# Weight subtractions, softmax scalings and unit-block additions on VectorE instead of GpSimd

## The chip, the core and the metric

The kernel runs on one NeuronCore of a Trainium2 chip. A core has a matmul engine (TensorE, PE in the rows; its weight loads are PEld), three engines for elementwise work (VectorE = DVE, ScalarE = ACT, GpSimd = POOL), a queue engine (SyncE = SP) and 16 DMA engines. The engines run their own instruction lists in order and wait for each other through semaphores. SBUF is the on-chip working memory, PSUM the memory into which TensorE writes its products. The metric is the device time of one execution in microseconds.

## The reference

Two transformer blocks run one after the other on 256 tokens of width 1024 in f32. Cut to what matters:

```python
# first block (16 meta tokens are put ahead of the 256)
z = rmsnorm(h, g_pre_mix) @ w_in
attn = sliding_window_attention_with_sinks(q, k, v, sinks)    # 8 heads of 64
hr = rg_lru(causal_depthwise_conv(xr), ...)                   # a scan along the tokens
h = h + rmsnorm(concat(attn, gelu(yr) * hr) @ w_out, g_post_mix)
h = h + rmsnorm(square(relu(rmsnorm(h, g_pre_ffn) @ w_ff1)) @ w_ff2, g_post_ffn)
# second block
proj = rms_norm(h, ln_pre_mix) @ w_in_2                       # 1024 -> 9232
y_a = moba_attention(rope(q_a), rope(k_a), v_a)               # 8 heads of 128
y_b = rms_norm(gated_delta_rule(q_b, k_b, v_b, g, beta)) * silu(z)   # a triangular solve per 64 tokens
merged = sigmoid(gate_a) * (y_a @ w_proj_a) + sigmoid(gate_b) * (y_b @ w_proj_b)
h = h + rms_norm(merged @ w_out_2, ln_post_mix)
h = h + rms_norm((silu(f @ w_gate) * (f @ w_up)) @ w_down, ln_post_ffn)   # f = rms_norm(h)
return h + sigmoid(h @ w_ple_gate) * rms_norm(p @ w_ple, ln_ple)
```

## The kernel before, in words

**Weights in two halves.** Every large product is computed as three matmuls in a reduced f32 format (fp32r): an operand x is split into `hi`, x rounded to fp32r, and `lo`, the rest x - hi, and the product is hi·hi + hi·lo + lo·hi (`mm3`). The weights arrive as 258 chunks of 128 x 1024, one DMA each, into a tile `raw` (4 buffers). `prep` splits a chunk in two halves of 512 columns; for each, a copy makes `whi` (ScalarE, sometimes VectorE, in the rows CAST) and a subtraction makes `wlo`. These are the 516 subtractions of the kernel: 436 on VectorE, 80 on GpSimd. Up to 9 chunks may be prepared ahead of the one in use. A chunk feeds 24 matmuls of 256 columns or 12 of 512.

**What sets the order.** The program is written out by a planner. Each call to an engine goes through `Timed` (so every row of the profile shows its line, 111), which moves a `Clock` of estimated times per engine and per tile. TensorE's list is mainly the weight stream. Between its pieces `tick` lets "side streams" (generators: attention, the delta rule, norms) advance when the Clock says that their tiles are ready, and `prefetch` prepares further chunks when the Clock's ACT, DVE and DMA times are not too far ahead of TensorE's. A change of the engine that does a step changes the estimates, and by them the place of many other steps in all lists.

**The steps that the change touches.** `split` gives a subtraction to GpSimd when GpSimd could start it more than 0.5 us (`PLO`) earlier than VectorE by the Clock. `softmax4` is used by both attentions: scores with mask into SBUF, row maximum, exponentials on ScalarE, reciprocal of the sum, then a scaling of four blocks, two of them on GpSimd. `gdn` is the delta rule of one pair of heads (four pairs, 0 to 3): GpSimd inverts 16 x 16 unit blocks by a chain of 14 pairs of small operations (`tmp`, `g`), sends them through DRAM into `cmp`, adds the unit diagonal (`cmp` + `eye`), and VectorE makes `Z` of it; GpSimd also makes the product `gm` for the next pair's decay, clears half of a tile `Q` (MEMSET) and computes powers (`aq`, `rk`, `ro`).

**Other names.** `u` is a normalised row block at the boundary between stages: VectorE makes it from `h`, a factor `ms` (a power, computed by GpSimd) and a gain, and TensorE transposes it into `uT`, on which the next weights act. `rope` multiplies a q or k pair by cosines and sines on VectorE (three rows `g<-ps,cst`), and GpSimd adds the two parts; `gl` holds the delta rule's log decays.

Of the kernel before, what the change touches and what calls it, by code (L numbers as in the profile page):

```python
# [8 lines left out]
F32 = mybir.dt.float32  # L9
# [39 lines left out]
WARM, KEEP = 8, (1, 1)  # L49
DHI, PLO, DCP = 0.0, 0.5, 1.0  # L50
FIRST = "x0 x1 x2 x3 k0 k1 q0 q1 y0 y1"
# [5 lines left out]
class Clock:  # L57
    """Estimated time of each engine and of each tile, by which the order of the program is chosen."""

# [27 lines left out]
class Soon(tuple):  # L87
    """Tiles that a stage of a side stream waits for, where it may be placed a little ahead of them."""


def parts_of(x):
    """Names under which the clock keeps a tile: the transposed operands in parts, others as a whole."""
    n = x.tensor.name
    if not n.startswith("uT"):
        return [n]
    dims = [d[1] for d in x.ap[1:]]
    (k, c), m = divmod(x.offset, TM), dims[0] if len(dims) > 1 else 1
    return [f"{n}.{i}.{j}" for i in range(k // 4, (k + m - 1) // 4 + 1) for j in range(c // P, (c + dims[-1] - 1) // P + 1)]


class Timed:
    """An engine whose calls also move the estimated times."""

# [41 lines left out]
def griffin_then_moba_gdn_kernel(ctx: ExitStack, tc, a, out):  # L145
# [54 lines left out]
    def copy(dst, src):  # L200
        on_dve = start_of("dve", src) + (DCP if src.tensor.name in clk.bank else DHI)
        if on_dve < start_of("act", src):
            dve.tensor_copy(dst, src)
        else:
            act.activation(dst, src, AF.Copy)

    def hilo(src, hi, lo, eng=None):
        copy(hi, src)
        (eng or dve).tensor_tensor(lo, src, hi.bitcast(F32), op=SUB)
# [21 lines left out]

# [1 line left out]
    jobs, posts, sides = [], [], []  # L233
# [17 lines left out]
    def split(i, j, src, hi, lo):  # L251
        if i < 2:
            return hilo(src, hi, lo, dve if (i, j) == (0, 1) else pool)
        copy(hi, src)
        eng = pool if start_of("pool", hi) + PLO < start_of("dve", hi) else dve
        eng.tensor_tensor(lo, src, hi.bitcast(F32), op=SUB)

# [87 lines left out]

# [1 line left out]
    def gain(n, scale=None, eng=dma):  # L347
# [80 lines left out]
    def tok_split(groups, after=None, cut=()):  # L428
        """Column groups of a product whose operand is still being made, token tile 0 before token tile 1."""
        def fn():  # L430
# [120 lines left out]
    def softmax4(parts, scale, sink, norm):  # L551
# [19 lines left out]
        for k, x in enumerate(norm):  # L571
            eng = pool if k < 2 else dve
            eng.tensor_scalar(x, x, sm[:, k:k + 1], None, op0=MUL)
        yield norm

# [1 line left out]
    hh = [hp.tile([P, D], F32, name=f"h{t}") for t in range(2)]  # L577
# [120 lines left out]

# [1 line left out]
    w1 = a["w1in"]  # L700
# [190 lines left out]

# [1 line left out]
    def hm4(t, r, hms):  # L893
# [57 lines left out]

# [1 line left out]
    beta, hbeta, gl, xx, eg, es = (small(n, (P, 2, 8)) for n in ("beta", "hbeta", "gl", "xx", "eg", "es"))  # L953
# [197 lines left out]
    def gdn(f, p):  # L1151
# [62 lines left out]
        yield cmp, aq  # L1214
        pool.tensor_tensor(cmp, cmp, bc4(C("eye")), op=ADD)
        dve.tensor_scalar(aq, aq, float(P) ** -0.5, None, op0=MUL)
# [128 lines left out]

# [1 line left out]
    def first2(hms):  # L1347
# [54 lines left out]

# [1 line left out]
    def fin(j):  # L1404
# [113 lines left out]
```

## Time and profile before

| | before |
|---|---|
| device time, three runs | 877.6, 879.09 (median), 881.04 us |
| profiled execution, first to last instruction | 878.8 us |
| TensorE busy | 849.5 us (97%) |
| VectorE busy | 610.7 us (69%) |
| ScalarE busy | 447.1 us (51%) |
| GpSimd busy | 278.1 us (32%) |
| mean granted TensorE clock | 0.992 |

The profiled execution's span lies 0.3 us below the median of the three runs. Busy time of TensorE is modelled at its ends, so 97% doesn't say that it streams all the time. The shares are means over stages that differ: 17 to 104 us is the first block's mixer, 123 to 295 its feed-forward part, 323 to 658 the second block's mixer, 663 to 856 its feed-forward part, and short boundaries lie between them.

### The profile page before, as it was taken

The numbers are of one execution on the slowest core, as the hardware profiler recorded it, in microseconds if no ns is written. First come the engines' busy times: TensorE is split into PE (matmuls) and PEld (weight loads), VectorE is DVE, ScalarE is ACT, GpSimd is POOL, SyncE is SP. The second block draws the span as 40 slices with busy tenths as digits, with TensorE's granted clock in tenths as the row PEclk, the third lists the DMA queues.
The fourth block names the chain that finished last, engine by engine and source line by source line (L and its number), as shares of the span: only waits on it lengthen the run. The fifth ranks groups of instructions, "written<-read, shape, count | busy, mean of one in ns | idle before, by whom it ended". The sixth has DMA issues, their size and how long they took to land.

```text
span 878.8 us, 15562 instructions
## 1 busy us (share of the span) xinstructions
PE 849.5 (97%) x5905; PEld 778.6 (89%) x5905; DVE 610.7 (69%) x1047; ACT 447.1 (51%) x995; POOL 278.1 (32%) x345
## 2 busy tenths in 40 slices
PE   8989989999999998899989999899999999999997
PEld 7978769999999788899989999899977999999977
DVE  6996887555555658988879998756758756645463
ACT  6855656554455454456444454346446545544441
POOL 4523321111111234454474758611223112311121
PEclk9999999999999999999999999999999999999999
DMA  7633737766665246444543335325553867565511
GB/s 275 232 124 116 253 106 255 240 186 185 184 189 191 74 165 212 131 143 130 201 132 122 99 107 193 114 88 172 183 168 129 270 199 268 190 197 187 188 53 49
DMA packets 47773, 147.19 MB, mean 167 GB/s; under 512 B 9281, under 2 KB 10561, under 8 KB 47698
## 3 DMA queue, kind: packets, MB, share of 16 engines
q1 hardware_dynamic: 47554, 146.13, 51.1%
q8 instruction: 46, 0.75, 0.3%
q14 instruction: 29, 0.24, 0.1%
q10 hardware_dynamic: 144, 0.07, 0.0%
HBM read 143.82 MB, written 2.36 MB: 166 GB/s over the span
## 4 chain that ended last, share of the span: by engine, by line
PE 73%; DVE 13%; POOL 6%; issue 4%; ACT 2%; DMA 2%; SPq 0%; DVEq 0%; POOLq 0%; ACTq 0%
PE ps L111 73%; DVE g L111 5%; DVE wlo L111 4%; POOL g L111 2%; POOL tmp L111 1%; DVE u L111 1%; DVE whi L111 1%; POOL sp_p L111 1%; ACT whi L111 1%; ACT junk L111 1%; DMA raw<-in_ff1t 1%; POOL wlo L111 1%; DVE s_m L111 1%; DMA g<-in_pT 0%; DMA raw<-in_w2q 0%
## 5 line engine op out<-in xcount | busy, mean ns | idle before, releaser
L111 PE MATMUL ps<-uT,whi 128*128 128x256 f32 (+1 forms) x2272 | 419.9, 286 | 0.0
L111 DVE TENSOR_TENSOR wlo<-raw,whi 128x512 fp32r<-128x512 f32 x436 | 320.3, 771 | 89.0 <-ACT whi L111 85.4
L111 PEld LDWEIGHTS ps<-uT,whi 128*128 128x128 f32 x2272 | 353.7, 190 | 4.7 <-issue 1.2
L111 ACT ACTIVATE whi<-raw 128x512 fp32r<-128x512 f32 x477 | 270.8, 623 | 110.1 <-issue 58.8
L111 PE MATMUL ps<-uT,wlo 128*128 128x256 f32 (+1 forms) x1136 | 320.4, 282 | 0.0
L111 PEld LDWEIGHTS ps<-uT,wlo 128*128 128x128 f32 x1136 | 216.4, 191 | 0.0
L111 POOL TENSOR_TENSOR wlo<-raw,whi 128x512 fp32r<-128x512 f32 x80 | 113.4, 1422 | 319.5 <-ACT whi L111 309.3
L111 PE MATMUL ps<-whi,hm 128*128 128x512 f32 x432 | 138.6, 393 | 0.0
L111 ACT ACTIVATE g<-ps 128x512 f32<-128x512 f32 (+4 forms) x104 | 51.6, 509 | 136.2 <-PE ps L111 132.1
L111 PEld LDWEIGHTS ps<-whi,hm 128*128 128x128 f32 x432 | 81.2, 188 | 17.4
L111 PE MATMUL ps<-g 128*128 128x128 f32 (+9 forms) x560 | 76.3, 287 | 11.2 <-POOL g L111 5.7
L111 PE MATMUL ps<-wlo,hm 128*128 128x512 f32 x216 | 84.9, 393 | 0.0
L111 PEld LDWEIGHTS ps<-g 128*128 128x128 f32 (+5 forms) x560 | 64.5, 181 | 17.8 <-POOL g L111 6.3
L111 PE MATMUL ps<-whi,uT 128*128 128x512 f32 (+1 forms) x256 | 74.6, 371 | 0.8 <-DVE uT L111 0.7
L111 PEld LDWEIGHTS ps<-whi,uT 128*128 128x128 f32 x256 | 45.5, 188 | 11.3 <-DVE uT L111 2.6
L111 POOL TENSOR_TENSOR g<-g 128x512 f32<-128x512 f32 (+1 forms) x20 | 30.6, 1531 | 72.7 <-DVE g L111 67.9
L111 PEld LDWEIGHTS ps<-wlo,hm 128*128 128x128 f32 x216 | 40.6, 188 | 8.3
L111 PE MATMUL ps<-wlo,uT 128*128 128x512 f32 (+1 forms) x128 | 46.9, 366 | 0.0
L111 DVE SCALAR_TENSOR_TENSOR g<-ps,vec,g 128x255 f32<-128x255 f32 (+5 forms) x84 | 35.0, 475 | 7.2 <-ACT g L111 6.9
L111 POOL TENSOR_TENSOR ms<-ms,mhalf 128x1 f32<-128x1 f32 (+1 forms) x19 | 11.7, 614 | 65.4 <-DVE ms L111 65.3
L111 ACT ACTIVATE junk<-ps 128x128 bf16<-128x128 f32 (+1 forms) x48 | 17.9, 384 | 27.5 <-PE ps L111 27.5
L111 ACT ACTIVATE hm<-g 128x512 fp32r<-128x512 f32 x23 | 14.6, 633 | 33.2 <-DVE g L111 33.2
(168 smaller groups left out, 905.2 us busy)
## 6 DMA issues: line engine op xcount, KB each, us to landing
raw<-in_ff SPq DMA_DIRECT2D x60, 512.0 KB, 4.4
raw<-in_w2qkv SPq DMA_DIRECT2D x24, 512.0 KB, 4.0
raw<-in_ffdown SPq DMA_DIRECT2D x22, 512.0 KB, 4.0
raw<-in_ffg SPq DMA_DIRECT2D x18, 512.0 KB, 4.3
raw<-in_ffu SPq DMA_DIRECT2D x18, 512.0 KB, 3.7
raw<-in_w1in SPq DMA_DIRECT2D x14, 512.0 KB, 3.6
raw<-in_w1out SPq DMA_DIRECT2D x8, 512.0 KB, 3.5
gain<-in_rows SPq DMA_DIRECT2D x16, 256.0 KB, 5.4
```

The lines of the kernel that those rows point to most:

```text
L111: r = call(*args, **kw)
```

## The change

Three kinds of operations go from GpSimd to VectorE: all subtractions for `wlo` but three in the first two chunks, the scaling of the first two blocks in `softmax4`, and the addition of the unit diagonal to `cmp`. The constant `PLO` goes with the rule that used it. Comments are dropped too.

```diff
-DHI, PLO, DCP = 0.0, 0.5, 1.0
+DHI, DCP = 0.0, 1.0
...
     def split(i, j, src, hi, lo):
-        if i < 2:
-            return hilo(src, hi, lo, dve if (i, j) == (0, 1) else pool)
-        copy(hi, src)
-        eng = pool if start_of("pool", hi) + PLO < start_of("dve", hi) else dve
-        eng.tensor_tensor(lo, src, hi.bitcast(F32), op=SUB)
+        hilo(src, hi, lo, pool if i < 2 and (i, j) != (0, 1) else dve)
...
         for k, x in enumerate(norm):
-            eng = pool if k < 2 else dve
-            eng.tensor_scalar(x, x, sm[:, k:k + 1], None, op0=MUL)
+            dve.tensor_scalar(x, x, sm[:, k:k + 1], None, op0=MUL)
...
         yield cmp, aq
-        pool.tensor_tensor(cmp, cmp, bc4(C("eye")), op=ADD)
+        dve.tensor_tensor(cmp, cmp, bc4(C("eye")), op=ADD)
```

Counted over the whole lists, VectorE's `wlo<-raw,whi` rows go from 436 to 513 and GpSimd's from 80 to 3; 16 scalings (8 of 128 x 128, 4 of 128 x 144, 4 of 128 x 256) and 4 additions of 128 x 64 change engine; and 8 `whi` copies that were VectorE's become ScalarE's, because the Clock now sees VectorE later. By stage, the 77 moved subtractions are 5 more on VectorE up to the end of the first mixer, 18 in the first feed-forward part, 27 in the second mixer, 25 in the second feed-forward part and 2 at the end. TensorE's and the DMA queue's instructions keep their number.

GpSimd's list from the end of the first mixer to the start of the second; `ms` is the power for a norm, of which each boundary has four. The difference of the lists:

```order
 L111 TENSOR_TENSOR g<-g 128x512 x4
-L111 TENSOR_TENSOR wlo<-raw,whi 128x512
-L111 TENSOR_TENSOR ms<-ms,mhalf 128x1 x4
-L111 TENSOR_TENSOR wlo<-raw,whi 128x512 x18
-L111 TENSOR_TENSOR ms<-ms,mhalf 128x1 x2
-L111 TENSOR_TENSOR wlo<-raw,whi 128x512
-L111 TENSOR_TENSOR ms<-ms,mhalf 128x1 x2
-L111 TENSOR_TENSOR wlo<-raw,whi 128x512 x2
+L111 TENSOR_TENSOR ms<-ms,mhalf 128x1 x8
 L111 TENSOR_TENSOR sp_s<-sp_s,sp_e 128x16
```

At both boundaries GpSimd is left with the eight powers alone.

GpSimd's list in the second mixer, where the small chain of head pair 0 ends and the `gm` of the next pair follows. Before:

```order
L111 TENSOR_TENSOR g<-g,cst 128x512
L111 TENSOR_TENSOR aq<-sq,mhalf 128x4
L111 TENSOR_TENSOR wlo<-raw,whi 128x512 x2
L111 TENSOR_TENSOR gm<-glr_106,cst 128x512
L111 TENSOR_TENSOR gm<-glr_107,cst 128x512
L111 TENSOR_TENSOR cmp<-cmp,cst 128x64
L111 MEMSET g 128x16x16
L111 TENSOR_TENSOR wlo<-raw,whi 128x512 x3
L111 TENSOR_TENSOR rk<-sk,mhalf 128x4
```

The same place after the change:

```order
L111 TENSOR_TENSOR g<-g,cst 128x512
L111 TENSOR_TENSOR aq<-sq,mhalf 128x4
L111 TENSOR_TENSOR gm<-glr_106,cst 128x512
L111 TENSOR_TENSOR gm<-glr_107,cst 128x512
L111 MEMSET g 128x16x16
L111 TENSOR_TENSOR rk<-sk,mhalf 128x4
```

The two subtractions ahead of `gm`, the addition behind it and three subtractions ahead of `rk` are gone.

VectorE's list at the second mixer's start, from the key's `rope` of the first attention pair (three products with `cst`) through that pair's softmax. Before:

```order
L111 TENSOR_TENSOR wlo<-raw,whi 128x512 x6
L111 TENSOR_TENSOR g<-ps,cst 128x512
L111 TENSOR_TENSOR g<-ps,cst 64x512 x2
L111 TENSOR_TENSOR wlo<-raw,whi 128x512 x5
L111 TENSOR_TENSOR g<-ps,cst 128x512
L111 TENSOR_TENSOR g<-ps,cst 64x512 x2
L111 SCALAR_TENSOR_TENSOR g<-ps,cst 128x256
L111 TENSOR_REDUCE s_m<-g 128x2
L111 SCALAR_TENSOR_TENSOR g<-ps,cst 128x512
L111 TENSOR_REDUCE s_m<-g 128x2
L111 TENSOR_SCALAR s_m<-s_m 128x4
L111 TENSOR_TENSOR wlo<-raw,whi 128x512 x2
```

After the change, from the row that follows that key's `rope`:

```order
L111 TENSOR_TENSOR wlo<-raw,whi 128x512 x4
L111 SCALAR_TENSOR_TENSOR g<-ps,cst 128x256
L111 TENSOR_REDUCE s_m<-g 128x2
L111 SCALAR_TENSOR_TENSOR g<-ps,cst 128x512
L111 TENSOR_REDUCE s_m<-g 128x2
L111 TENSOR_SCALAR s_m<-s_m 128x4
L111 TENSOR_TENSOR g<-ps,cst 128x512
L111 TENSOR_TENSOR g<-ps,cst 64x512 x2
L111 CAST whi<-raw 128x512
L111 TENSOR_TENSOR wlo<-raw,whi 128x512 x2
L111 RECIPROCAL s_r<-s_r 128x4
L111 TENSOR_SCALAR g<-g,s_r 128x128 x2
```

Between the query's `rope` and the key's stand 3 subtractions where there were 6; between the key's `rope` and the scores stand 4 where there were 5, and the next pair's query `rope` has moved behind the scores. The two scalings of 128 x 128 are new on this engine.

## Rows read from the trace of the kernel before

**Rows 1.** The page's first part: busy us, share of the span, instructions.

```profile
PE 849.5 (97%) x5905; PEld 778.6 (89%) x5905; DVE 610.7 (69%) x1047; ACT 447.1 (51%) x995; POOL 278.1 (32%) x345
```

**Rows 2.** Busy time by stretch; behind the engines the granted clock, DMA share, GB/s.

```profile
17.00:60.00 43.00, 39.03 (x303) 37.26 (x303) 40.95 (x74) 30.48 (x66) 19.66 (x33) 1.00 0.58 200
...
123.00:295.00 172.00, 172.00 (x1076) 155.09 (x1077) 96.34 (x148) 89.50 (x166) 24.44 (x17) 1.00 0.63 202
323.00:361.00 38.00, 33.08 (x257) 31.73 (x255) 33.71 (x53) 20.35 (x45) 20.25 (x31) 0.99 0.61 208
...
455.00:491.00 36.00, 36.00 (x298) 35.22 (x298) 33.77 (x70) 18.94 (x50) 15.60 (x19) 0.95 0.37 119
491.00:530.00 39.00, 38.40 (x330) 38.04 (x328) 36.22 (x85) 17.27 (x61) 25.14 (x45) 1.00 0.35 109
530.00:564.00 34.00, 31.26 (x251) 29.94 (x250) 27.09 (x47) 15.06 (x43) 28.97 (x56) 0.95 0.46 148
```

**Rows 3.** Groups by form: count, then busy us, mean ns, idle before.

```profile
L111 DVE TENSOR_TENSOR wlo<-raw,whi 128x512 fp32r<-128x512 f32 x436 | 320.3, 771 | 89.0 <-ACT whi L111 85.4
...
L111 POOL TENSOR_TENSOR wlo<-raw,whi 128x512 fp32r<-128x512 f32 x80 | 113.4, 1422 | 319.5 <-ACT whi L111 309.3 <-PE ps L111 5.9 <-issue 3.0
...
L111 DVE CAST whi<-raw 128x512 fp32r<-128x512 f32 x39 | 22.2, 570 | 2.8 <-PE ps L111 2.8
```

**Rows 4.** VectorE's timeline while GpSimd has no large operation: start, us, what.

```profile
111.09 1.41 DVE L111 SCALAR_TENSOR_TENSOR u<-h,ms,gain 128x512 f32<-128x512 f32 x2 [0.67 <-POOL ms L111]
...
685.74 0.69 DVE L111 TENSOR_TENSOR wlo<-raw,whi 128x512 fp32r<-128x512 f32 x1 [1.14 <-ACT whi L111]
...
690.51 1.90 DVE L111 TENSOR_TENSOR wlo<-raw,whi 128x512 fp32r<-128x512 f32 x3
```

**Rows 5.** Timeline at three boundaries; in brackets idle time before and its releaser.

```profile
117.63 3.45 DVE L111 SCALAR_TENSOR_TENSOR u<-h,ms,gain 128x512 f32<-128x512 f32 x2 [0.66 <-POOL ms L111]
121.14 0.66 PE L111 MATMUL ps<-ident,u 128*128 128x128 f32 x4 [1.02 <-DVE u L111]
122.94 0.50 PE L111 MATMUL ps<-whi,uT 128*128 128x512 f32 x1 [0.68 <-DVE uT L111]
...
298.18 1.29 PE L111 MATMUL ps<-ident,u 128*128 128x128 f32 x8 [0.61 <-DVE u L111]
...
657.51 2.52 DVE L111 SCALAR_TENSOR_TENSOR u<-h,ms,gain 128x512 f32<-128x512 f32 x2
657.52 1.29 POOL L111 TENSOR_TENSOR wlo<-raw,whi 128x512 fp32r<-128x512 f32 x1 [0.40 <-POOL ms L111]
659.50 1.29 PE L111 MATMUL ps<-ident,u 128*128 128x128 f32 x8 [0.67 <-DVE u L111]
```

**Rows 6.** Timeline from 450 to 455 us, GpSimd and TensorE.

```profile
450.14 2.51 POOL L111 TENSOR_TENSOR wlo<-raw,whi 128x512 fp32r<-128x512 f32 x2
453.70 0.49 PE L111 MATMUL ps<-gm,mgt 128*128 128x512 f32 x1 [2.08 <-POOL gm L111]
454.71 0.50 PE L111 MATMUL ps<-gm,mgt 128*128 128x512 f32 x1 [0.51 <-POOL gm L111]
```

**Rows 7.** Timeline from 548 to 554 us, GpSimd and TensorE.

```profile
548.64 1.28 POOL L111 TENSOR_TENSOR wlo<-raw,whi 128x512 fp32r<-128x512 f32 x1
...
553.64 1.08 PE L111 MATMUL ps<-g 128*128 128x64 f32 x8 [1.81 <-POOL g L111]
```

**Rows 8.** Timeline of the second mixer's start, VectorE and TensorE.

```profile
335.47 0.59 PE L111 MATMUL ps<-gl,cst 128*128 128x16 f32 x4 [1.05 <-DVE gl L111]
347.68 1.58 PE L111 MATMUL ps<-g 128*128 128x128 f32 x8 [1.53 <-POOL g L111]
...
354.56 2.38 DVE L111 TENSOR_TENSOR wlo<-raw,whi 128x512 fp32r<-128x512 f32 x2
360.84 0.58 PE L111 MATMUL ps<-g 128*128 128x128 f32 x1 [2.33 <-POOL g L111]
```

**Rows 9.** Timeline in the first mixer, TensorE's longest wait.

```profile
59.73 2.73 PE L111 MATMUL ps<-g 64*128 64x144 f32 x16 [3.62 <-ACT g L111]
```

More of the change, by code (lines that the diff above doesn't have):

```diff
@@ L87 @@
 class Soon(tuple):
+    pass
 def parts_of(x):
```

## The prediction

> **What bounds the kernel now.** I read the page's busy times first, then the stretches, then in the timelines each place where TensorE waits. TensorE is busy for 849.5 of 878.8 us and VectorE for 610.7 [rows 1]. So at most about 29 us of shown idle time, and what the clock gives back, can be won, while VectorE as a whole has room. By stretch that is different [rows 2]: in the feed-forward part from 123 to 295 us TensorE has no idle time at all and VectorE uses 96.34 of 172 us; in the mixers VectorE is nearly full (40.95 of 43 us, 33.71 of 38, then 33.77 of 36 and 36.22 of 39), and TensorE's waits lie there and at the boundaries. The reader should see two kinds of wait: behind VectorE, at the boundaries [rows 5] and at the mixers' starts [rows 8, 9], and behind GpSimd's list, in the delta rule [rows 6, 7].
>
> **What a subtraction costs on either engine.** On GpSimd one takes 1.42 us [rows 3]. On VectorE a lone one shows 0.69 us and three in a row 1.90 us, so one adds about 0.63 us [rows 4]. But GpSimd's are not free for VectorE. Two `u` operations take 1.41 us where GpSimd does nothing large [rows 4], and 2.52 us where a GpSimd subtraction begins within 0.01 us of them; at 117.63 us, beside two GpSimd subtractions, 3.45 us [rows 5]. One GpSimd subtraction thus stretches a VectorE operation with two SBUF operands by 1.1 us (2.52 - 1.41), which is more than the 0.63 us that doing it on VectorE costs. It shows in the mean too: VectorE's 436 subtractions take 771 ns where a lone one takes 690, which is 35 us in all [rows 3, 4], from all of GpSimd's large operations together.
>
> The Trainium skill (SBUF — State Buffer, section Who interferes with whom) has a rule for this: a VectorE instruction with two SBUF inputs and a GpSimd instruction that reads SBUF take turns at one shared port, and the loser is blocked for the whole instruction. The stretched `u` rows agree. By that rule alone the change relieves VectorE wherever both engines meet, and costs it 0.63 us wherever they don't.
>
> **The change part by part.**
>
> 1. *77 subtractions to VectorE:* 77 x 0.63 = 48.5 us added, 77 x 1.42 = 109 us off GpSimd. 43 of them lie in the two feed-forward parts. There they are 27 us beside a VectorE that is busy 56% of the time (96.34 of 172): hidden, and taken as 0; without that room it would be up to 27 us.
>
> 2. *The relief:* between 0 (no subtraction meets a two-operand instruction) and 77 x 1.1 = 85 us (all do). The 35 us above, shared with GpSimd's other work, lead me to 25 us.
>
> 3. *16 scalings and 4 additions:* VectorE's price for these widths isn't shown apart. Bounds: 0.16 us each (a quarter of the 512-wide 0.63 us, for 128 wide) and 0.63 us, so 3 to 13 us; I take 6, nearer the width. The 8 copies that leave VectorE take 8 x 0.57 = 4.6 us with them [rows 3]. Net, VectorE's busy time goes from 610.7 to about 636 us (610.7 + 48.5 - 25 + 6 - 4.6), between 605 and 668.
>
> 4. *First mixer, 17 to 60 us:* VectorE works there without a pause, so what counts is its sum. Five subtractions come to it by the lists (+3.2 us), and up to five collisions of 1.1 us leave (-5.5 us); I take 0, between -2.3 and +3.2. The longest wait of TensorE, 3.62 us at 59.73 [rows 9], is for a ScalarE copy queued behind exponentials that wait for VectorE. It stays. The eight scalings here come after it, in a stretch with room.
>
> 5. *Boundaries:* GpSimd's list has only the powers left there (first piece of the lists), so the `u` operations fall back to 1.41 us a pair. TensorE waits 1.02 and 0.68 us at the first, 0.61 at the second and 0.67 at the third [rows 5], each smaller than the stretch that goes (2.04, 1.1, 1.1 us). Sum -3.0 us, bounds 0 and -3.0. What is late next is the chain of norm and power itself, which isn't touched.
>
> 6. *The next pair's `gm`:* two subtractions of 2.51 us stand ahead of it in GpSimd's list, and TensorE waits 2.08 and 0.51 us for it [rows 6]. After the change `gm` follows `aq` at once (second piece): -2.5 us, bounds 0 and -2.6.
>
> 7. *The MEMSET for `Q`:* TensorE waits 1.81 us for it at 553.64, and a 1.28 us subtraction stands in the small chain ahead of it [rows 7]: -1.3 us. Against this, the new list puts pair 2's MEMSET behind the whole small chain of pair 3, where it stood inside; TensorE's order has the matmul that needs it only shortly ahead of pair 3's own. Bounds -1.8 and +3.
>
> 8. *The clock behind these waits:* behind the waits of 6 and 7 the granted clock is 0.95 over 36 and over 34 us [rows 2], that is, some microseconds at 1.2 GHz, which cost 1.8 and 1.7 us. Where the wait goes the loss may go; I take half, -1.75 us, bounds 0 and -3.5.
>
> 9. *Second mixer's start, 323 to 361 us:* TensorE waits 1.05, 1.53 and 2.33 us, first for the decays, then for the first two pairs' `rope` [rows 8]. Of the second mixer's 27 moved subtractions about three belong here by time (27 x 38 / 335; +1.9 us), with four scalings; a pair that shows 2.38 us here instead of 1.32 [rows 4, 8] loses its 1.1 us stretch. The third piece of the lists matters more: the key's `rope` now stands three subtractions (1.9 us) earlier, and scores behind 7 instead of 11. The decays' matmuls stand 21 weight matmuls later. I take -1.5 us, bounds +2 and -4.9.
>
> 10. *The rest of the second mixer:* VectorE is fullest from 455 to 530 us (70.0 of 75 us). By time six moved subtractions belong there (27 x 75 / 335; +3.8 us), less what is relieved. I take +1.0 us, bounds 0 and +5.
>
> Sum: -3.0 - 2.5 - 1.3 - 1.75 - 1.5 + 1.0 = -9.05, so 878.8 - 9.05 = 869.8 us; I predict 870. The profiled execution lies 0.3 us below the median, which changes nothing here. The DMA queue issues the same transfers.
>
> **The rivals.**
>
> *The waits move on (no change).* TensorE's list is rewritten by a planner whose estimates don't know the collisions. It now believes VectorE to be later, so the places of attention and delta rule shift by up to three chunks, and each shifted piece may meet another unfinished operand. For it: waits in the mixers go with VectorE's fill, which hardly falls (610.7 to 636 us overall). Against it: the boundary waits and `gm` aren't places where anything else is late by as much. Keeping 3 to 4 us of the gain at the boundaries and losing the rest gives 876, with new waits 880 us.
>
> *VectorE becomes the wait (slower).* The three full stretches (17 to 60, 323 to 361, 455 to 530) get 5 + 3 + 6 = 14 of the moved subtractions by the counts above. They and 12 scalings add 14 x 0.63 + 12 x 0.3 = 12.4 us to a VectorE that has 11.4 us of gaps there (2.05 + 4.29 + 5.01), gaps that are mostly waits of its own. If nothing is relieved and the gaps can't be used, the 12.4 us land on TensorE and only the boundaries' 3 us come back: 888 us. It decides where the relief per moved subtraction falls under 0.63 us, that is, where fewer than six in ten meet a two-operand instruction. For it: at the mixers many VectorE operations read PSUM, and those need not meet. Against it: the 35 us of stretch.
>
> The Trainium skill (Perfetto Trace Analysis, section Optimizing Scalar/DVE Operations) speaks for this rival: a saturated VectorE may be helped by work given to ScalarE or even GpSimd, which this change takes back. The same paragraph warns that between VectorE and GpSimd it might not help because of the shared port. The stretched rows bear out the warning more than the advice.
>
> **How the numbers follow.** Three runs before lie within 3.4 us, so 0.5% (4.4 us) is about what can be told from no change: faster is under 874.7, slower over 883.5. The forecast with its own range (863 to 877) has 0.64, the waits that move on 0.24 (876 to 882), VectorE as the wait 0.12 (882 to 890). Of the forecast's 0.64 a small part lies above 874.7, about 0.05; of the slower rival 0.03 ends below 883.5. So faster 0.59, same 0.32, slower 0.09. All lower bounds together (-2.3 - 3.0 - 2.6 - 1.8 - 3.5 - 4.9) give 861; under 862 I leave 0.07, and over 881 0.12, which makes the range 862 to 881 us.
>
> **What would show it.** Right: three rows for GpSimd's `wlo`; VectorE's `wlo` mean at 0.70 to 0.74 us instead of 0.77; `u` pairs at the boundaries at 1.4 us; no wait for `gm` over 0.5 us and a clock of 1.00 behind it; VectorE busy near 636 us and GpSimd under 169 (278.1 - 109). Wrong: waits for VectorE of over 2 us at new places in 323 to 564 us; a MEMSET that TensorE waits for behind pair 3's chain; a mean of VectorE's subtractions that stays at 0.77, since then GpSimd's other operations were the cause.

## The result, and the profile after

| | before | after |
|---|---|---|
| device time, median (lowest to highest) | 879.18 us (877.6 to 881.04) | 865.5 us (864.2 to 866.18) |
| ratio, 95% interval | | 0.9834 (0.9813 to 0.9855) |
| span of the profiled execution | 878.8 us | 864.0 us |
| mean granted TensorE clock | 0.992 | 0.994 |

The change saves 13.7 us by the medians; the sum of the prediction gave 9.05. The first part of the page after the change answers to [rows 1]:

```profile
PE 848.0 (98%) x5905; PEld 777.2 (90%) x5905; DVE 620.3 (72%) x1135; ACT 449.9 (52%) x1004; POOL 160.0 (19%) x248
```

GpSimd gave up 118 us (278.1 to 160.0), and VectorE took up only 9.6 (610.7 to 620.3). The groups by form after the change show the exchange (busy us, mean ns; answers to [rows 3]):

```profile
L111 DVE TENSOR_TENSOR wlo<-raw,whi 128x512 fp32r<-128x512 f32 x513 | 349.4, 724 | 85.8 <-ACT whi L111 83.2
...
L111 DVE CAST whi<-raw 128x512 fp32r<-128x512 f32 x31 | 15.5, 500 | 0.5 <-PE ps L111 0.4
...
L111 DVE SCALAR_TENSOR_TENSOR u<-h,ms,gain 128x512 f32<-128x512 f32 x12 | 8.5, 746 | 0.4 <-POOL ms L111 0.4
```

Seventy-seven more subtractions cost VectorE 29.1 us (349.4 - 320.3), that is, 0.38 us each and not 0.63, because their mean became shorter: 724 ns where it was 771. The 31 remaining copies take 500 ns where 39 took 570.

To see where the time came from, the program has to be cut at the same matmuls in both traces. I cut at the transposes of `u` at the second and third boundary, which start at 298.18 and 659.50 us before [rows 5] and at 296.50 and 644.63 us after. The busy times in the first two of the three stretches of the kernel before (length; then busy PE, PEld, DVE, ACT, POOL; then the granted clock):

```profile
0.00:298.18 298.18, 285.36 (x1779) 250.57 (x1780) 200.10 (x342) 169.32 (x351) 72.15 (x82) 0.99 0.59 190
...
298.18:659.50 361.32, 349.75 (x2718) 333.44 (x2719) 284.91 (x518) 173.96 (x446) 161.06 (x226) 0.99 0.45 145
```

The same two after the change:

```profile
0.00:296.50 296.50, 289.02 (x1780) 252.00 (x1781) 202.93 (x372) 168.74 (x351) 31.52 (x50) 0.99 0.59 191
...
296.50:644.63 348.13, 345.03 (x2720) 330.41 (x2718) 284.32 (x549) 177.23 (x454) 118.47 (x187) 1.00 0.47 151
```

Nearly all of the gain lies in the second mixer: 361.32 to 348.13, or 13.2 us. TensorE's idle time there fell from 11.6 to 3.1 us (length less busy), and its busy time by 4.7 us; the clock, 1.00 instead of 0.99, makes about 3.5 of that (my estimate, 1% of 349.75). VectorE's busy time there did not rise: 284.91 before, 284.32 after, with 31 more instructions. The stretch up to the second boundary gives 1.7 us, the one behind the third nothing (219.30 and 219.42).

### The profile page after: what moved, and what is told of

Read it like the earlier page. It is cut to its first block, busy times and chain, and to the rows that moved or that the text cites. A ratio compares the mean times of both kernels' runs of the same rounds, so it can differ in the third digit from the quotient of the medians.

```text
span 864.0 us, 15454 instructions
## 1 busy us (share of the span) xinstructions
PE 848.0 (98%) x5905; PEld 777.2 (90%) x5905; DVE 620.3 (72%) x1135; ACT 449.9 (52%) x1004; POOL 160.0 (19%) x248
## 4 chain that ended last, share of the span: by engine, by line
PE 80%; DVE 7%; POOL 5%; DMA 3%; ACT 3%; issue 2%; SPq 0%; POOLq 0%; ACTq 0%; DVEq 0%
PE ps L111 80%; POOL g L111 3%; DVE g L111 2%; DVE wlo L111 2%; POOL tmp L111 2%; ACT g L111 1%; ACT whi L111 1%; DVE s_m L111 1%; DMA raw<-in_w1in 1%; DMA raw<-in_ff1t 1%; DMA xmt<-in_meta 1%; DVE whi L111 0%; DMA gain<-in_rows 0%; DVE u L111 0%; POOL aq L111 0%
## 5 line engine op out<-in xcount | busy, mean ns | idle before, releaser
L111 DVE TENSOR_TENSOR wlo<-raw,whi 128x512 fp32r<-128x512 f32 x513 | 349.4, 724 | 85.8 <-ACT whi L111 83.2
L111 ACT ACTIVATE whi<-raw 128x512 fp32r<-128x512 f32 x485 | 275.3, 622 | 101.3 <-issue 65.2
L111 PE MATMUL ps<-g 128*128 128x128 f32 (+9 forms) x560 | 73.0, 278 | 3.1 <-ACT g L111 1.9
L111 PEld LDWEIGHTS ps<-g 128*128 128x128 f32 (+5 forms) x560 | 62.6, 176 | 9.3 <-issue 3.1
L111 DVE SCALAR_TENSOR_TENSOR g<-g,ps 128x512 f32<-128x512 f32 x23 | 15.7, 681 | 17.3 <-ACT g L111 14.3
```

What stands on the lines that cost most here:

```text
L111: r = call(*args, **kw)
```

## The experiments

All ratios are to the kernel before, run on the same chip (its medians were 881.1, 880.9 and 881.2 us in the three groups of runs).

| kernel | us | ratio (95%) |
|---|---|---|
| old plan, subtractions on VectorE | 873.8 | 0.9930 (0.9907 to 0.9952) |
| new plan, subtractions on GpSimd | 880.2 | 0.9995 (0.9985 to 1.0004) |
| subtractions alone, planned anew | 866.4 | 0.9842 (0.9826 to 0.9859) |
| scalings and additions alone, planned anew | 885.8 | 1.0063 (1.0036 to 1.0090) |
| scalings and additions alone, old plan | 879.3 | 0.9986 (0.9971 to 1.0001) |
| changed kernel + GpSimd reads | 887.6 | 1.0066 (1.0043 to 1.0088) |
| changed kernel + GpSimd writes | 871.3 | 0.9893 (0.9876 to 0.9909) |
| before, planner charges the stretch | 878.6 | 0.9982 (0.9971 to 0.9994) |
| before, one estimate changed | 882.6 | 1.0023 (1.0011 to 1.0035) |
| changed kernel, the same estimate changed | 866.7 | 0.9846 (0.9825 to 0.9868) |
| changed kernel + two more kinds of additions on VectorE | 869.2 | 0.9856 (0.9828 to 0.9883) |
| the same + the delta rule's products on VectorE | 861.2 | 0.9767 (0.9748 to 0.9785) |

### Engines or plan?

A change of the engine also rewrites the plan. Since a `Timed` wrapper has an engine and a name under which the Clock charges it, the two can be separated.

Old plan, subtractions on VectorE:

```diff
+    as_pool = Timed(clk, nc.vector, "pool")
...
-        eng = pool if start_of("pool", hi) + PLO < start_of("dve", hi) else dve
+        eng = as_pool if start_of("pool", hi) + PLO < start_of("dve", hi) else dve
```

> The plan of before is kept row for row on every engine (the Clock still charges GpSimd), but the 77 subtractions run on VectorE; scalings and additions stay on GpSimd. Theory 'engines' (the gain is collisions and GpSimd's queue): 866 to 871 us, with the u pairs at the boundaries at 1.4 us and the wait at the MEMSET gone. Theory 'plan' (the gain is the new order of TensorE's pieces): 876 to 880 us.

New plan, the 77 subtractions on GpSimd (`GPS` is the list of them):

```diff
+    as_dve = Timed(clk, nc.gpsimd, "dve")
...
-        hilo(src, hi, lo, pool if i < 2 and (i, j) != (0, 1) else dve)
+        hilo(src, hi, lo, pool if i < 2 and (i, j) != (0, 1) else as_dve if (i, j) in GPS else dve)
```

> The plan of the changed kernel is kept, but the 77 subtractions that GpSimd did before run on GpSimd again (the Clock charges VectorE). Theory 'engines': 876 to 881 us, with u pairs stretched to 2.5 us and more. Theory 'plan': 865 to 869 us.

Neither alone is the change. The engines under the old plan bring 0.70% (873.8 us, between the ranges of both theories), the plan with the old engines 0.05%, and both together 1.58% (subtractions alone) to 1.66%. But the 0.05% is not a plan without effect. Cut at the same transposes as above, one execution of each kernel gives (us; the third row's execution took 1.5 us more than its kernel's median):

| | to the second boundary | second mixer | behind the third |
|---|---|---|---|
| before | 298.18 | 361.32 | 219.30 |
| old plan, subtractions on VectorE | 297.41 | 354.64 | 218.95 |
| new plan, subtractions on GpSimd | 302.76 | 356.07 | 221.17 |
| changed kernel | 296.50 | 348.13 | 219.42 |

In the second mixer the engines alone bring 6.7 us and the plan alone 5.3, which is nearly the 13.2 of both. Outside it the new plan loses 6.5 us as long as GpSimd subtracts, and nothing when VectorE does. Two groups of TensorE's matmuls show what each part takes away: products with `g` of 128 x 128, among them those that wait for `rope` [rows 8], and the transposes of `u`. Behind the second bar stands TensorE's idle time before them, with its releasers. Before:

```profile
L111 PE MATMUL ps<-g 128*128 128x128 f32 x240 | 33.6, 280 | 4.2 <-POOL g L111 3.9 <-DVE g L111 0.4
...
L111 PE MATMUL ps<-ident,u 128*128 128x128 f32 x64 | 10.1, 281 | 6.2 <-DVE u L111 6.1
```

Old plan, subtractions on VectorE:

```profile
L111 PE MATMUL ps<-g 128*128 128x128 f32 x240 | 32.7, 276 | 3.4 <-POOL g L111 3.2
...
L111 PE MATMUL ps<-ident,u 128*128 128x128 f32 x64 | 9.7, 294 | 3.4 <-DVE u L111 3.4
```

New plan, subtractions on GpSimd:

```profile
L111 PE MATMUL ps<-g 128*128 128x128 f32 x240 | 32.3, 275 | 0.6 <-POOL g L111 0.6
...
L111 PE MATMUL ps<-ident,u 128*128 128x128 f32 x64 | 10.7, 299 | 6.6 <-DVE u L111 6.6
```

After the change, both:

```profile
L111 PE MATMUL ps<-g 128*128 128x128 f32 x240 | 32.2, 275 | 0.6 <-POOL g L111 0.6
...
L111 PE MATMUL ps<-ident,u 128*128 128x128 f32 x64 | 9.4, 284 | 1.7 <-DVE u L111 1.5
```

The waits for `u` shrink with the subtractions on VectorE, the waits for `rope`'s sums [rows 8] go with the new plan. The stretched `u` pair of [rows 5], 3.45 us at 117.63, takes 1.42 us under the old plan too (at 118.45), but the MEMSET's wait [rows 7] is hardly smaller there:

```profile
547.81 1.08 PE L111 MATMUL ps<-g 128*128 128x64 f32 x8 [1.59 <-POOL g L111]
```

Why the new plan loses time outside the second mixer while GpSimd subtracts was not tried apart.

### Which part of the change?

Subtractions alone:

```diff
-            dve.tensor_scalar(x, x, sm[:, k:k + 1], None, op0=MUL)
+            eng = pool if k < 2 else dve
+            eng.tensor_scalar(x, x, sm[:, k:k + 1], None, op0=MUL)
...
-        dve.tensor_tensor(cmp, cmp, bc4(C("eye")), op=ADD)
+        pool.tensor_tensor(cmp, cmp, bc4(C("eye")), op=ADD)
```

> Only the subtractions move, with the plan that follows; scalings and additions stay on GpSimd. Both theories expect most of the gain here: 865 to 869 us. A rival, that the scalings matter (two on GpSimd ahead of the probability transposes), expects 871 us or more.

Scalings and additions alone, on the kernel before: the same lines the other way round.

> Only the 16 scalings and the 4 additions move; the subtractions are placed by the old rule. If these are a small part of the change: 876 to 881 us. The rival that they carry a third or more of the gain expects under 874.5 us.

The subtractions carry the change; the rest adds nothing that can be told (0.9842 against 0.9834), and alone, planned anew, it loses 0.63%, where I had expected 876 to 881 us. To see whether the 20 operations or the plan lose it, the same move was made under the old plan:

```diff
-            eng = pool if k < 2 else dve
+            eng = as_pool if k < 2 else dve
...
-        pool.tensor_tensor(cmp, cmp, bc4(C("eye")), op=ADD)
+        as_pool.tensor_tensor(cmp, cmp, bc4(C("eye")), op=ADD)
```

> The kernel before, with its plan row for row, but the 16 softmax scalings and the 4 additions run on VectorE (the planner still charges them to GpSimd); the subtractions stay where they were. The kernel that made the same move and was planned anew was 0.63% slower. Theory: these few small operations cost next to nothing either way (20 operations of 0.2 to 0.4 us against two-operand relief of the same order), so 878 to 883 us, and the loss of the replanned kernel came from its other plan, which pushed gm and a g of the delta rule into collisions. Rival: the operations themselves delay VectorE in the full mixers, 884 to 888 us.

At 0.9986 the operations themselves cost nothing. The loss is the new plan's. Its trace shows two places. In the first, a subtraction (450.99) has come to stand inside GpSimd's small chain, an operation of the chain shows 1.87 us (452.86) beside three subtractions of VectorE, and TensorE waits 3.78 us for `gm` (before 2.08). In the second, VectorE's scaling of `sq`, 128 x 4, shows 2.75 us beside two subtractions of GpSimd, and TensorE waits 3.15 us for a `g` that VectorE makes later in its list. Over the whole kernel TensorE's waits for `gm` sum to 4.3 us instead of 2.6, those for VectorE's `g` to 6.6 instead of 1.9.

```profile
450.99 1.30 POOL L111 TENSOR_TENSOR wlo<-raw,whi 128x512 fp32r<-128x512 f32 x1
...
452.78 1.89 DVE L111 TENSOR_TENSOR wlo<-raw,whi 128x512 fp32r<-128x512 f32 x3
...
452.86 1.87 POOL L111 TENSOR_TENSOR tmp<-g 32x14 f32<-32x14 f32 x1
...
458.29 0.50 PE L111 MATMUL ps<-gm,mgt 128*128 128x512 f32 x1 [3.78 <-POOL gm L111]
...
540.69 2.75 DVE L111 TENSOR_SCALAR sq<-sq 128x4 f32<-128x4 f32 x1
540.90 2.51 POOL L111 TENSOR_TENSOR wlo<-raw,whi 128x512 fp32r<-128x512 f32 x2
...
546.08 0.71 PE L111 MATMUL ps<-g 128*128 128x128 f32 x4 [3.15 <-DVE g L111]
```

### Is it the reading, or GpSimd's list?

GpSimd is made busy again at the 77 places, once with an operation that reads two operands of 128x512, once with operations that mostly write. Both are added to the changed kernel, and their results go to a scratch tile that nothing uses.

```diff
+        if (i, j) in GPS:
+            nc.gpsimd.tensor_tensor(scr, hi.bitcast(F32), hi.bitcast(F32), op=ADD)
```

> The changed kernel, with a GpSimd operation added at each of the 77 places that the subtractions left: a 128x512 addition of hi to itself into a scratch tile, whose result nobody uses. VectorE still makes wlo, and the planner doesn't know of the additions, so the plan is that of the changed kernel. Theory (what GpSimd's subtractions cost was the stretch of VectorE's two-operand operations beside them, and unplanned lateness by it): the stretch returns, VectorE's wlo mean goes from 724 to 750 ns or more, and the time goes from 865.5 to 873 to 881 us. Rival A (GpSimd's list was the cost: the small chains behind the subtractions): also slower, by 4 to 12 us, so that this kernel alone doesn't tell; read it against the one that only writes. Rival B (the gain is the plan alone, wherever things run): 864 to 868 us.

```diff
+        if (i, j) in GPS:
+            nc.gpsimd.tensor_scalar(scr[:, 0:1], hi.bitcast(F32)[:, 0:1], 1.0, None, op0=MUL)
+            for _ in range(2):
+                nc.gpsimd.memset(scr, 0.0)
```

> The changed kernel, with GpSimd occupied at the same 77 places for about as long, but without reading operands of that size: one addition-like operation on a single column of hi (so that it starts when the subtraction would have) and two memsets of a 128x512 scratch tile. Results unused, plan that of the changed kernel. Theory (the stretch of VectorE is the cost): wlo's mean stays within 15 ns of 724, the u pairs at the boundaries stay at 1.4 us, and the time stays at 865 to 869 us. Rival A (GpSimd's list is the cost): as slow as the kernel with the reading additions, 870 to 878 us, with waits of TensorE for gm and for the MEMSET of Q.

Here is the same place, the first boundary, in both. With reads:

```profile
120.91 3.06 DVE L111 SCALAR_TENSOR_TENSOR u<-h,ms,gain 128x512 f32<-128x512 f32 x2
120.93 2.49 POOL L256 TENSOR_TENSOR scr<-whi 128x512 f32<-128x512 f32 x2 [0.36 <-ACT whi L111]
```

With writes:

```profile
119.90 1.41 DVE L111 SCALAR_TENSOR_TENSOR u<-h,ms,gain 128x512 f32<-128x512 f32 x2
...
120.78 1.11 POOL L258 MEMSET scr<- 128x512 f32 x2
```

And the groups of `wlo` on VectorE and of the added operations, with reads:

```profile
L111 DVE TENSOR_TENSOR wlo<-raw,whi 128x512 fp32r<-128x512 f32 x513 | 371.3, 767 | 68.3 <-ACT whi L111 65.7
L256 POOL TENSOR_TENSOR scr<-whi 128x512 f32<-128x512 f32 x77 | 99.2, 1288 | 341.6 <-ACT whi L111 321.9 <-DVE whi L111 19.3
```

With writes:

```profile
L111 DVE TENSOR_TENSOR wlo<-raw,whi 128x512 fp32r<-128x512 f32 x513 | 347.8, 721 | 85.7 <-ACT whi L111 82.9
L258 POOL MEMSET scr<- 128x512 f32 x154 | 81.1, 527 | 9.0
L256 POOL TENSOR_SCALAR scr<-whi 128x1 f32<-128x1 f32 x77 | 41.6, 541 | 320.4 <-ACT whi L111 301.4 <-DVE whi L111 18.3
```

The writes occupy GpSimd longer (81.1 + 41.6 = 122.7 against 99.2 us) and leave `wlo` at 721 ns and the `u` pair at 1.41 us. The reads bring back 767 ns and 3.06 us. VectorE's whole busy time says the same: 620.3 us in the changed kernel, 622.5 with the writes, 659.9 with the reads. So the 77 reads add 39.6 us to it, 0.51 us each. Both kinds hold `whi` longer (ScalarE waits 15.9 us for the reads and 22.4 us for the writes), so that is not the difference. In time, GpSimd's occupation costs about 5 us (0.9893 over 0.9834 is 0.6%), 2 more than I had allowed it; the reading costs 16 us more (887.6 - 871.3), also more than I had expected, since here VectorE keeps the 77 subtractions and bears the stretch on top. So most of what GpSimd's subtractions cost was the stretch of VectorE, and a smaller part GpSimd's list. The list's part lies ahead of the second mixer: that mixer takes 348.13 us in the changed kernel, 348.29 with the writes and 358.42 with the reads. In the first mixer the added writes stand ahead of two products of GpSimd for which VectorE's scan then waits 2.59 us, and TensorE's wait of [rows 9], 1.93 us after the change, becomes 3.83:

```profile
48.45 3.69 DVE L111 TENSOR_TENSOR_SCAN g<-g 128x272 f32<-128x272 f32 x4 [2.59 <-POOL g L111]
```

### Is the new plan a lucky one, and could the old one have known?

One number of the Clock is changed, in the kernel before and in the changed one:

```diff
-                cost = 0.07 + (0.52e-3 if op == "tensor_copy" and ins[0] not in self.clock.bank else 1.04e-3) * m
+                cost = 0.08 + (0.52e-3 if op == "tensor_copy" and ins[0] not in self.clock.bank else 1.04e-3) * m
```

> The kernel before with one number of the planner changed: the fixed part of its estimate for each VectorE operation is 0.08 instead of 0.07 us. Nothing on any engine is changed in kind; the order of the lists is. It measures what an arbitrary other plan is worth, beside which the 0.63% of the kernel with only the scalings and additions moved, and part of the gain of the change itself, may be chance of the plan. Theory (a plan is worth some microseconds by chance): off by 2 to 6 us from before, in either direction. Rival (plans of near-equal estimates run alike): within 2 us of before.

> The changed kernel with the same number of the planner changed, 0.08 instead of 0.07 us. If the gain of the change comes from its engines, this kernel lies within 4 us of the changed one (862 to 870 us) and well below the kernel before under the same number. Rival (the changed kernel's plan is a lucky one): 872 to 880 us.

In both kernels the engines' lists are reordered at some 200 places, and the times move by 0.23% and 0.12% (0.9846 against 0.9834). These two other plans are worth 1 to 2 us; the scalings and additions planned anew show that a plan can cost more (1.0063 against 0.9986 with the same engines, about 7 us). The gain of 13.7 us is twice that and stays under the other estimate, so that a lucky plan doesn't explain it, though part of it is the plan's.

Then the kernel before, with a Clock that charges VectorE for each subtraction given to GpSimd:

```diff
         eng.tensor_tensor(lo, src, hi.bitcast(F32), op=SUB)
+        if eng is pool:
+            clk.now["dve"] += 0.45
```

> The kernel before, with every engine as it was and the same rule, but the planner's clock adds 0.45 us to VectorE for each subtraction that it gives to GpSimd (36 us of stretch of VectorE beside GpSimd's subtractions, over 80 of them). If the loss of before is mainly a plan that doesn't know the collisions, a plan that knows their mean price wins part of it back without moving a single step by hand: 868 to 877 us. Rival (a mean price is no help, since a collision hits one operand at one place and lateness there can't be planned for; only taking the collisions away helps): 878 to 886 us.

It gains 0.18%, no more than another plan does. This doesn't settle the point: a VectorE that looks later makes the rule give GpSimd more, 107 subtractions instead of 80, and the mean on VectorE rose to 813 ns. Cut as above, its second mixer is 4.8 us shorter (356.52), and the stretch behind the third boundary 2.0 us longer (221.31).

### Can it be taken further?

In the changed kernel GpSimd still makes the additions in `rope` and behind a projection's product, the masking products `g<-g,cst` and `gm`. First the additions go to VectorE, then the others too:

```diff
-        pool.tensor_tensor(dst, dst, tmp, op=ADD)
+        dve.tensor_tensor(dst, dst, tmp, op=ADD)
...
-            pool.tensor_tensor(tg, tg, S2["ma"][c], op=ADD)
+            dve.tensor_tensor(tg, tg, S2["ma"][c], op=ADD)
```

> The changed kernel, and the additions of GpSimd in rope and behind the first projection's product go to VectorE too; planned anew. About 28 us of stretch are left on VectorE in the changed kernel, most of it beside these additions. Theory (each removed collision makes the plan truer and relieves VectorE): 857 to 863 us. Rival (the mixers' VectorE is full from 323 to 361 us and 491 to 530 us, so now the added 0.6 us apiece land on TensorE): 865 to 873 us.

```diff
-                        pool.tensor_tensor(gm[i].rearrange("p (h t n) -> p h t n", h=2, t=2),
+                        dve.tensor_tensor(gm[i].rearrange("p (h t n) -> p h t n", h=2, t=2),
...
-        pool.tensor_tensor(a3(atT, 4), a3(atT, 4), bc4(C("mle")), op=MUL)
+        dve.tensor_tensor(a3(atT, 4), a3(atT, 4), bc4(C("mle")), op=MUL)
...
-        pool.tensor_tensor(a3(X, 4), a3(A, 4), bc4(C("nsl")), op=MUL)
+        dve.tensor_tensor(a3(X, 4), a3(A, 4), bc4(C("nsl")), op=MUL)
...
-        pool.tensor_tensor(a3(M, 4), a3(A, 4), bc4(C("lvl")), op=MUL)
+        dve.tensor_tensor(a3(M, 4), a3(A, 4), bc4(C("lvl")), op=MUL)
```

> As the kernel before this one, and GpSimd's last 128x512 operations with two operands (gm and the three masking products of the delta rule) go to VectorE as well; planned anew. Then nothing large of GpSimd reads SBUF beside VectorE but the first chunks. Theory: stretch near 0, waits for gm (1.27 and 0.69 us in the changed kernel) gone, 853 to 861 us. Rival: VectorE's list in the delta rule becomes the wait, with TensorE waiting over 1 us several times for DVE in 424 to 564 us, 866 to 876 us.

The first step alone gains nothing (0.9856; its interval overlaps the changed kernel's), as its rival had it (865 to 873 us). With both, the kernel is 2.3% below before and, by the two ratios, 0.7% below the changed one. Its page:

```profile
PE 842.1 (98%) x5905; PEld 774.0 (90%) x5905; DVE 619.4 (72%) x1161; ACT 452.9 (53%) x1010; POOL 113.2 (13%) x216
```

Its group of `wlo` on VectorE:

```profile
L111 DVE TENSOR_TENSOR wlo<-raw,whi 128x512 fp32r<-128x512 f32 x513 | 335.7, 697 | 82.2 <-ACT whi L111 79.7
```

Its second mixer, between the same matmuls as above:

```profile
294.65:637.50 342.85, 342.60 (x2719) 329.14 (x2718) 283.00 (x575) 180.11 (x460) 72.18 (x155) 1.00 0.48 153
```

VectorE has 26 instructions more than in the changed kernel and is busy for less (619.4 against 620.3); `wlo` is at 697 ns, the lone one's 0.69 us [rows 4]; in the second mixer TensorE is idle for 0.25 of 342.85 us. That is the best version here. What TensorE still idles lies ahead of the second mixer (8.8 us) and behind it (5.4 us).

## Why the prediction was right, and where its sizes were off

The mechanism held: GpSimd's reads stretch VectorE's operations, and without them the waits at the boundaries and most of those in the second mixer go. The added reads and writes show it in isolation. Only the comparison with which it began doesn't hold in the mean: a `u` row that meets a subtraction loses 1.1 us, but over the whole kernel a subtraction on GpSimd cost VectorE 0.5 us, a little less than the 0.63 us of doing it. Three GpSimd subtractions are left, `wlo` fell into the range named (724 ns of 700 to 740), and the boundaries' `u` pairs are at 1.41 us. Between the two profiled executions 14.8 us went (878.8 to 864.0), against 9.05 forecast, and the difference lies in the second mixer: the terms for it (step 6 to 10 and 0.67 us of step 5) sum to -6.7 us, and it gave -13.2. Three of the signs named for being right failed: TensorE still waits 1.27 us for `gm`, the clock behind that is 0.97, and VectorE is busy for 620.3 us and not near 636. (The lower end of 605 that step 3 gives for it doesn't follow from the bound of 85 us on the relief, by which it would be 573.)

**Steps 1 and 2, subtractions and relief.** In the feed-forward parts nothing was lost: TensorE stays busy for all of 123 to 295 us, and the stretch behind the third boundary has the same length. The relief was mis-sized. VectorE rose by 9.6 us instead of 25. With the forecast's own terms for what was added and removed (48.5 + 6 - 4.6 = 49.9), the relief is 49.9 - 9.6 = 40 us where I took 25. Two runs give about the same without those terms: under the old plan, with the subtractions alone moved, VectorE rose by 10.6 us (621.3) instead of 48.5, a relief of 38, and the 77 added reads brought 39.6 back. I had started from the stretch in the subtractions' mean alone; the 12 `u` operations (1271 ns before, 746 after, 6.3 us in all) and the copies were stretched too. Per subtraction that is 0.52 us over the whole kernel, under the 0.63 from which the rival "VectorE becomes the wait" decides. But its place is the full mixers, and in the second one 27 more subtractions left VectorE's busy time as it was (284.91 and 284.32 us), so that the relief there paid for them; elsewhere it rose, by 2.8 us up to the second boundary and by 7.3 behind the third, where VectorE had room.

**Step 3** was about right: under the old plan the 20 scalings and additions alone raise VectorE's busy time by 4.8 us (615.5), their own relief included, where I took 6 without it, and the device time doesn't rise.

**Step 4, first mixer.** The net was near 0 as taken (the first boundary's transposes come at 111.27 instead of 111.98 us), but "It stays" was wrong: the wait of 3.62 us [rows 9] became 1.93. The matmul begins 0.97 us earlier, and TensorE ran dry 0.72 us later.

```profile
58.76 1.41 PE L111 MATMUL ps<-g 64*128 64x144 f32 x14 [1.93 <-ACT g L111]
```

**Step 5, boundaries.** The waits of [rows 5] went or shrank to what comes next, a ScalarE copy of `uT`:

```profile
117.45 1.41 DVE L111 SCALAR_TENSOR_TENSOR u<-h,ms,gain 128x512 f32<-128x512 f32 x2
121.22 0.50 PE L111 MATMUL ps<-whi,uT 128*128 128x512 f32 x1 [0.25 <-ACT uT L111]
...
296.50 1.04 PE L111 MATMUL ps<-ident,u 128*128 128x128 f32 x8
...
644.63 1.03 PE L111 MATMUL ps<-ident,u 128*128 128x128 f32 x8
```

Yet the stretch up to the second boundary gained 1.7 us and not the 2.3 of its terms: 5.3 us of idle time went (12.8 to 7.5), and TensorE's busy time rose by 3.7 us. The clock makes about 1.5 of that: from 86 to 123 us it fell (3.3 us, below), while from 60 to 86 us it rose from 0.93 to 1.00 (1.8 us). The rest is not explained.

**Step 6, `gm`.** The lists did what was said: `gm` starts as `aq` ends. But the wait did not go.

```profile
443.82 1.01 POOL L111 TENSOR_TENSOR aq<-sq,mhalf 128x4 f32<-128x4 f32 x1
444.81 2.44 POOL L111 TENSOR_TENSOR gm<-glr,cst 128x512 fp32r<-128x512 f32 x2
446.12 0.50 PE L111 MATMUL ps<-gm,mgt 128*128 128x512 f32 x1 [1.27 <-POOL gm L111]
```

The matmul begins 1.3 us behind the end of `aq`; before, 3.56 us (453.70 - 450.14). TensorE came to this place 6.8 us earlier (it ran dry at 444.85, before at 451.62), the small chain 5.3 us earlier. I had asked what the wait is for, but not how much earlier TensorE would come.

**Step 7, MEMSET.** The whole wait of 1.81 us went. The new place of pair 2's MEMSET, behind pair 3's chain, brought no wait: from 496 to 600 us TensorE idles for 0.30 us.

**Step 8, clock.** In sum the forecast was met, but by chance, since the places were others. What the clock holds back over the span fell from 7.0 us (0.8% of 878.8) to 5.2 (0.6% of 864.0). To compare places, I cut at the `gm` product of step 6, at the next pair's `gm` product and at the first product with `ybT`. Before:

```profile
453.70:504.42 50.72, 50.21 (x414) 49.12 (x415) 47.01 (x99) 24.09 (x68) 27.65 (x43) 0.97 0.37 121
504.42:613.76 109.34, 106.00 (x897) 103.15 (x895) 82.85 (x165) 52.77 (x153) 49.89 (x83) 0.98 0.42 134
```

After the change:

```profile
446.12:496.26 50.14, 49.45 (x409) 48.33 (x409) 42.53 (x94) 22.25 (x65) 19.80 (x31) 0.97 0.30 95
496.26:599.63 103.37, 103.07 (x890) 100.73 (x889) 88.13 (x185) 55.34 (x158) 45.33 (x82) 1.00 0.51 162
```

Behind the wait for `gm`, which stayed, nothing came back: 0.97 in both. (From 455 to 491 us the clock is 0.95 before and 1.00 after only because the same work lies earlier now: from 424 to 455 us it is 1.00 before and 0.94 after.) Behind the MEMSET's wait, which went, all of it came back, not half. Ahead of `gm` the clock rose from 0.99 to 1.00, which no term had, and in the first mixer's tail it fell. The stretches after the change that this and the next step rest on:

```profile
86.00:123.00 37.00, 33.78 (x135) 24.75 (x134) 30.06 (x48) 22.30 (x48) 5.99 (x6) 0.91 0.44 146
323.00:361.00 38.00, 37.41 (x302) 36.50 (x301) 33.65 (x59) 18.14 (x47) 15.24 (x27) 1.00 0.51 167
...
491.00:530.00 39.00, 38.95 (x334) 38.68 (x333) 38.25 (x81) 21.70 (x69) 28.31 (x52) 1.00 0.47 144
```

**Steps 9 and 10** were mis-sized most. TensorE's idle time from 323 to 361 us fell from 4.92 to 0.59 us, or by 4.3, where I took 1.5; that is near the bound of 4.9 that I had named. Part of this is the plan's and not the relief's, since the waits for `rope`'s sums went with the new plan on the old engines too. Step 10 had forecast a loss of 1.0 us: from 455 to 491 us TensorE had no idle time before and has none now, and from 491 to 530 us it fell from 0.60 to 0.05 us. So the moved subtractions cost TensorE nothing there. The relief is the term behind that: I added the moved subtractions at 0.63 us and subtracted a stretch only where I saw a row, while the second mixer's VectorE total stayed level.

**The rival "the waits move on"** had a true core. The plan moves waits by microseconds: alone it brings 5.3 us in the second mixer and loses 6.5 outside it, and the loss is gone when VectorE subtracts. That the new plan loses nothing then *because* its estimates come true without the collisions is my reading; the kernel whose Clock was told of the stretch doesn't decide it. The rival "VectorE becomes the wait" was to decide where the relief per moved subtraction falls under 0.63 us. It did (0.5 us), but the difference lies where VectorE has room.

## What to carry to other kernels

Price an operation on GpSimd with what it takes from VectorE, not only with its own time: here one 128x512 subtraction there cost VectorE 0.5 us of stretch, against 0.63 us for doing it. Measure the relief over a whole stretch cut at the same instructions (VectorE's busy time of the second mixer stayed at 285 us), not from the one group that shows it best. Where a planner writes the order, run the engines' change and the plan's change apart, compare them stage by stage and not only in sum, since a gain and a loss can cancel, and try more than one other plan to know what a plan is worth.

## What the runs showed of the hardware that was not expected

**A tiny operation can be held for microseconds.** VectorE's scaling of `aq`, 128 x 4, with a single operand in SBUF, takes 0.16 us and once, before the change, 3.90 us, while GpSimd ran two subtractions (to 452.65 us) and two `gm` products. All four of its kind, before (the view of one tile; ns: shortest, median, longest; then the first and last start):

```profile
L111 DVE TENSOR_SCALAR aq<-aq x4: 161/194/3897, 451.3 to 566.5; 128x4 f32<-128x4 f32 x4
```

The scaling of `sq` shown above, 2.75 us in the kernel with the scalings and additions planned anew, is another.

The Trainium skill (SBUF — State Buffer, section Who interferes with whom) lists copies, casts and `tensor_scalar` among the operations that can take the shared port in their two-port modes; this row and the copies' mean (570 to 500 ns) agree. The same section says that a GpSimd instruction that only writes does not contend with a VectorE instruction with two SBUF inputs; the kernel with memsets agrees (721 ns).

**It goes both ways.** GpSimd's small operations of the unit-block chain take twice their time (0.62 us instead of 0.28) while VectorE runs subtractions. After the change, five subtractions from 433.03 to 436.6 us, and the chain beside and behind them:

```profile
433.03 3.60 DVE L111 TENSOR_TENSOR wlo<-raw,whi 128x512 fp32r<-128x512 f32 x5 [3.14 <-ACT whi L111]
...
435.46 0.62 POOL L111 TENSOR_TENSOR tmp<-g 32x56 f32<-32x56 f32 x1
...
437.23 0.28 POOL L111 TENSOR_TENSOR g<-g,tmp 32x54 f32<-32x54 f32 x1
```

So the chain that `gm` follows is not relieved by the change: from its `g<-g,tmp` 32 x 14 to the end of `aq` it takes 14.8 us (from 430.07), before 14.3 (from 435.87).

**The clock fell where TensorE idled no more than before.** Windows of 4 us after the change (granted clock in the third number from the end):

```profile
92.00:96.00 4.00, 2.61 (x9) 1.30 (x8) 4.00 (x8) 2.56 (x5) 0.00 (x0) 0.99 0.56 185
96.00:100.00 4.00, 4.00 (x11) 2.64 (x10) 3.50 (x6) 2.30 (x4) 0.00 (x0) 0.58 0.82 286
```

And before:

```profile
108.00:112.00 4.00, 1.77 (x9) 1.15 (x7) 1.91 (x5) 2.32 (x8) 0.55 (x1) 1.00 0.34 110
112.00:116.00 4.00, 3.94 (x19) 2.72 (x20) 3.84 (x7) 1.81 (x4) 0.55 (x1) 1.00 0.00 0
```

After the change, a window in which TensorE was busy for 2.61 of 4 us is followed by 0.58, that is, mostly the lower level of 1.2 GHz; before, one with 1.77 us was followed by 1.00. From 86 to 123 us the clock is 0.91 after the change and 1.00 before, about 3.3 us (37 x 0.09) lost there. What decided it is not shown, and it was not tried apart.
